# A hybrid retention and attention layer on one core: half of the projection's block pairs by seven products

## The chip, the cores and the metric

One core of a Trainium2 chip runs the whole layer. The metric is the device time of one execution in microseconds (us). TensorE multiplies matrices into the eight banks of PSUM, VectorE (DVE) and ScalarE (ACT) do elementwise work, GpSimd (POOL) and SyncE (SP) issue most DMAs.

## The reference

The input x has 256 rows (tokens) of 4096. It is normalised to h, and one product `proj = h @ w_in` gives 24,592 columns: q, k, v and gate of a retention branch (4 x 2048), q, k, v and gate of a forgetting attention (4 x 2048), 16 forget logits and 2 x 4096 merge gates. Then:

```
y_r = groupnorm(retention(rotary(q_r), rotary(k_r), v_r)) * silu(g_r)      (8 heads of 256)
y_f = softmax(q_f k_f^T / sqrt(128) + decay of the forget logits) v_f * silu(g_f)  (16 heads of 128)
merged = sigmoid(gate_0) * (y_r @ w_branch_ret) + sigmoid(gate_1) * (y_f @ w_branch_fox)
out = layernorm(2**0.25 * h + merged @ w_out)
```

All weights are float32: w_in is 403 MB, the two branch matrices 34 MB each, w_out 67 MB.

## The kernel before

Tokens lie on the output's partitions: two token tiles of 128. Every large product is cut into chunks of 512 columns, and a chunk into units of two blocks of 128 rows of weights (`KG = 2`), 512 KB each. `add_chunk` (line 100) lists the units of all chunks in the order of the work: 17 chunks of gate columns (the first with the forget logits, two narrow ones at the end), 16 chunks of retention (q, k, v, gate for each of four groups), 16 of forgetting attention, 16 of the two branch products, 8 of the output product.

The product is float32 in three rounded parts. `u_split` (line 116) makes of a raw weight block a high part (a copy that rounds, line 125, on ScalarE) and a low part (raw minus high, line 126, on VectorE). h has the parts hTh and hTl. `u_pe` (line 130) then issues for each block and token tile three matmuls of 512 columns into the same accumulator: high by high (line 144), low weight by high h (line 145), high weight by low h (line 146). A unit of full width is 2 x 2 x 3 = 12 matmuls.

`u_load` (line 110) loads a unit on SP's queue into one of five raw buffers. The split parts have four buffers of 128x512 each (`RING * KG`). `feed` (line 690) emits the splits of a unit once the unit two before it has its last step behind it. The emitted order is not the final one: when the program is built, each engine's queue is ordered by a list scheduler that takes the instruction that is ready. Where a run of units takes the token tiles one after the other (the first four and the last five units), `keep_for` (line 669) gives them other buffers.

In the first 16 units the input's normalisation, transposes and splits (`hT_part`, line 191) run between the units.

At the end of a chunk an evacuation takes the accumulator (two banks for both token tiles, two such pairs). For gates (line 248) it adds a bias, takes the sigmoid and stores to `gates_d` in device memory on POOL's queue. For q and k of retention it multiplies by cosine and sine (lines 297, 300) and combines (307, 308); for the others it copies. What remains of attention (transposes, scores, softmax or group norm, products) is written as Python generators in the list `bg`, and `bg_step` (line 151) runs one or two of their steps after each unit, so that attention of a group runs under the projection of the next. The merge chunks fetch gates from `gates_d`, multiply (lines 521, 531, 532), transpose; the output chunks add the residual, prepared in `pre` (lines 587 to 590), in `ev` (lines 596 to 601).

Four PSUM banks belong to the accumulators (`accp`), four to everything else (`psp`).

Of the kernel before, what the change touches and what calls it, by code (L numbers as in the profile page):

```python
# [8 lines left out]
F32 = mybir.dt.float32  # L9
# [15 lines left out]
KG = 2  # L25
EPS = 1e-5
ALPHA = 2.0 ** 0.25
BIG = 3.0e38


@with_exitstack
def hybrid_kernel(
# [16 lines left out]
    accp = ctx.enter_context(tc.tile_pool(name="accp", bufs=2, space=PS))  # L49
# [4 lines left out]
    cumT_d = dram.tile([FH, S], F32, name="cumT_d")  # L54

# [40 lines left out]
    units = []  # L96
    where = dict(w_in=0, w_branch_ret=0, w_branch_fox=0, w_out=0)
    RING, LOADS = 2, 5

    def add_chunk(wname, n, stat, evac, drain_at=None, pre=None, apart=False):  # L100
        ng = len(stat) // KG
        holder = {}
        for g in range(ng):
            size = KG * P * n
            w0 = where[wname]
            where[wname] += size
            units.append(dict(src=aps[wname][w0:w0 + size], n=n, stat=stat, g=g, ng=ng, evac=evac, h=holder,
                              drain=g == drain_at, pre=pre if g == 4 else None, keep=None, apart=apart))

    def u_load(u):  # L110
        n = u["n"]
        raw = wp.tile([P, KG * NC], F32, name="wraw", tag="wraw", bufs=LOADS)
        nc.sync.dma_start(raw[:, :KG * n], u["src"].rearrange("(p f) -> p f", p=P))
        u["raw"] = raw[:, :KG * n].rearrange("p (j n) -> p j n", j=KG)

    def u_split(u):
        n = u["n"]
        u["hi"], u["lo"] = [], []
        for j in range(KG):
            if u["keep"] is None:  # L120
                hi = wp.tile([P, NC], F32R, name="whi", tag="whi", bufs=RING * KG)
                lo = wp.tile([P, NC], F32R, name="wlo", tag="wlo", bufs=RING * KG)
            else:
                hi, lo = u["keep"][j]
            u["copy"] = nc.scalar.copy(hi[:, :n], u["raw"][:, j, :]).ins  # L125
            nc.vector.tensor_tensor(lo[:, :n], u["raw"][:, j, :], hi[:, :n].bitcast(F32), op=ALU.subtract)  # L126
            u["hi"].append(hi)
            u["lo"].append(lo)

    def u_pe(u, tiles):  # L130
        n, g = u["n"], u["g"]
        if "acc" not in u["h"]:
            a = accp.tile([P, T, NC], F32, name="acc", tag="acc")
            b = accp.tile([P, T, NC], F32, name="acc", tag="acc") if u["apart"] else a
            u["h"]["acc"], u["h"]["by"] = a, (a, b)
        by = u["h"]["by"]
        for j in range(KG):
            sh, sl, k = u["stat"][g * KG + j]
            first = g == 0 and j == 0
            last = g == u["ng"] - 1 and j == KG - 1  # L140
            for t in tiles:
                ts = slice(t * P, (t + 1) * P)
                o = by[t][:, t, :n]
                nc.tensor.matmul(o, lhsT=sh[:, k, ts], rhs=u["hi"][j][:, :n], start=first, stop=False)  # L144
                nc.tensor.matmul(o, lhsT=sh[:, k, ts], rhs=u["lo"][j][:, :n], start=False, stop=False)  # L145
                mm = nc.tensor.matmul(o, lhsT=sl[:, k, ts], rhs=u["hi"][j][:, :n], start=False, stop=last)  # L146
        return mm.ins
# [43 lines left out]
    def hT_part(blocks, t0, t1):  # L191
        """Transposes, scales, shifts and splits the given k blocks of token tiles t0..t1 (one bank)."""
# [55 lines left out]
    def gate_evac(a0, off, n):  # L248
        def f(acc):
# [3 lines left out]
            if off:  # L253
                fz = work.tile([P, T, FH], F32, name="fz", tag="fz", bufs=1)
                nc.vector.tensor_tensor(
                    fz, acc[:, :, 0:FH], bforg[:, None, :].to_broadcast([P, T, FH]), op=ALU.add
                )
                bg.append(forget_bg(fz))
            nc.vector.tensor_tensor(
                g[:, :, :n], acc[:, :, off:off + n], bb[:, None, :n].to_broadcast([P, T, n]), op=ALU.add  # L260
            )
# [7 lines left out]
    yrh = big.tile([P, 16, S], F32R, name="yrh", tag="yb0")  # L269
    yrl = big.tile([P, 16, S], F32R, name="yrl", tag="yb1")  # L270
# [13 lines left out]

    def ret_group(gi):
        st = {}

        def ev_rot(name):
            def f(acc):
                if not rscr:  # L290
                    rscr["ab"] = big.tile([P, 4, T, NC], F32, name="rab", tag="yb2")
                    rscr["ry"] = big.tile([P, 4, T, NC], F32, name="rry", tag="yb3")
                pi = 0 if name == "q" else 1
                A, B = rscr["ab"][:, 2 * pi], rscr["ab"][:, 2 * pi + 1]
                for t in range(T):
                    v = acc[:, t, :].rearrange("p (a b) -> p a b", b=P)
                    nc.vector.tensor_tensor(
                        A[:, t, :].rearrange("p (a b) -> p a b", b=P), v,
                        cos[:, t, None, :].to_broadcast([P, 4, P]), op=ALU.mult)
                    nc.vector.tensor_tensor(  # L300
                        B[:, t, :].rearrange("p (a b) -> p a b", b=P), v,
                        sin[:, t, None, :].to_broadcast([P, 4, P]), op=ALU.mult)
                R = rscr["ry"][:, pi].rearrange("p t (h x b) -> p t h x b", h=2, x=2)
                Av = A.rearrange("p t (h x b) -> p t h x b", h=2, x=2)
                Bv = B.rearrange("p t (h x b) -> p t h x b", h=2, x=2)
                for t in range(T):
                    nc.vector.tensor_tensor(R[:, t, :, 0, :], Av[:, t, :, 0, :], Bv[:, t, :, 1, :], op=ALU.subtract)
                    nc.vector.tensor_tensor(R[:, t, :, 1, :], Bv[:, t, :, 0, :], Av[:, t, :, 1, :], op=ALU.add)
                dst = work.tile([P, 4, S], F32, name=name, tag="at_" + name, bufs=1)
                st[name] = dst  # L310

                def cb(i0, ps):
                    nc.scalar.copy(dst[:, i0:i0 + 2, :], ps)

                bg.append(transpose_to(cb, lambda i, t: R[:, t, i // 2, i % 2, :], 4))
            return f

        def ev_v(acc):
            v = work.tile([P, T, NC], F32, name="v", tag="at_v", bufs=1)
            nc.scalar.copy(v, acc)  # L320
            st["v"] = v

        def ev_g(acc):
# [522 lines left out]
```

## Time and profile before

| | us |
|---|---|
| two runs | 2918.99 and 2919.61, median 2919.3 |
| span of the profiled execution | 2917.6 |
| median less that span | 1.7 |

The profile is of one execution. Its own time outside the span is not listed; the span and the 1.7 us up to the median stand for it. In the page and in what was asked of the trace, L12 is line 12 of the kernel, "out<-in" names tiles, a mean is that of one instruction, and "<-" behind an idle time names what ended it. Matmuls are pipelined: one is recorded at 0.39 us although the next begins earlier.

### The profile page before, as it was taken

The numbers are of one execution on the slowest core, as the hardware profiler recorded it, in microseconds if no ns is written. First come the engines' busy times: TensorE is split into PE (matmuls) and PEld (weight loads), VectorE is DVE, ScalarE is ACT, GpSimd is POOL, SyncE is SP. The second block draws the span as 40 slices with busy tenths as digits, with TensorE's granted clock in tenths as the row PEclk, the third lists the DMA queues.
The fourth block names the chain that finished last, engine by engine and source line by source line (L and its number), as shares of the span: only waits on it lengthen the run. The fifth ranks groups of instructions, "written<-read, shape, count | busy, mean of one in ns | idle before, by whom it ended". The sixth has DMA issues, their size and how long they took to land.

```text
span 2917.6 us, 37002 instructions
## 1 busy us (share of the span) xinstructions
PE 2888.2 (99%) x13146; PEld 2399.4 (82%) x13146; DVE 1689.5 (58%) x2622; ACT 1402.0 (48%) x2326; POOL 110.0 (4%) x198
## 2 busy tenths in 40 slices
PE   7999999999999999999999999999999999999998
PEld 5888888889888888888888888888888888888886
DVE  7555555555555555555555555555556656666666
ACT  5544444445444444444445454555455444444443
POOL 0000000000000000000000001000000000000000
PEclk9999999999999999999999999999999999999999
DMA  6666666666656566565666656666666666666674
GB/s 222 215 217 205 214 214 205 216 214 189 219 181 199 183 198 189 181 197 182 198 188 184 189 182 192 192 186 187 187 196 205 213 215 211 220 216 226 214 230 174
DMA packets 164394, 586.88 MB, mean 201 GB/s; under 512 B 19259, under 2 KB 19531, under 8 KB 164203
## 3 DMA queue, kind: packets, MB, share of 16 engines
q1 hardware_dynamic: 151632, 543.49, 57.7%
q0 software_dynamic: 12000, 38.93, 5.1%
q8 instruction: 102, 1.67, 0.2%
q10 hardware_dynamic: 576, 2.10, 0.2%
q14 instruction: 84, 0.69, 0.1%
HBM read 571.76 MB, written 12.68 MB: 200 GB/s over the span
## 4 chain that ended last, share of the span: by engine, by line
PE 98%; DVE 1%; DMA 1%; ACT 0%; issue 0%; SPq 0%; DVEq 0%; ACTq 0%
PE acc L146 32%; PE acc L145 32%; PE acc L144 32%; PE ps L279 1%; DMA x<-in_x 1%; DVE z L637 0%; DMA wraw<-in_w_out 0%; PE ps L434 0%; PE ps L345 0%; DVE wlo L126 0%; PE ps L200 0%; PE ps L451 0%; ACT whi L125 0%; PE ps L461 0%; PE ps L462 0%; PE ps L348 0%
## 5 line engine op out<-in xcount | busy, mean ns | idle before, releaser
L126 DVE TENSOR_TENSOR wlo<-wraw,whi 128x512 fp32r<-128x512 f32 (+2 forms) x2070 | 1406.3, 683 | 1152.8 <-ACT whi L125 1151.9
L125 ACT CAST whi<-wraw 128x512 fp32r<-128x512 f32 (+2 forms) x2070 | 1272.5, 617 | 1441.0 <-DVE wlo L126 1116.7
L145 PE MATMUL acc<-wlo,hTh 128*128 128x512 f32 (+2 forms) x3128 | 1214.6, 388 | 0.2 <-DVE wlo L126 0.2
L144 PE MATMUL acc<-whi,hTh 128*128 128x512 f32 (+2 forms) x3128 | 1210.4, 387 | 2.1 <-DVE hTh L206 2.1
L146 PE MATMUL acc<-whi,hTl 128*128 128x512 f32 (+2 forms) x3128 | 1205.2, 385 | 0.6 <-DVE rstd L91 0.6
L144 PEld LDWEIGHTS acc<-whi,hTh 128*128 128x128 f32 x3128 | 588.0, 188 | 119.7 <-ACT whi L125 2.5
L146 PEld LDWEIGHTS acc<-whi,hTl 128*128 128x128 f32 x3128 | 588.2, 188 | 116.3 <-DVE hTl L207 1.1
L145 PEld LDWEIGHTS acc<-wlo,hTh 128*128 128x128 f32 x3128 | 588.1, 188 | 115.9 <-DVE wlo L126 0.8
L145 PE MATMUL acc<-wlo,mTh 128*128 128x512 f32 x500 | 194.7, 389 | 0.4 <-DVE wlo L126 0.4
L146 PE MATMUL acc<-whi,mTl 128*128 128x512 f32 x500 | 194.5, 389 | 0.0
L144 PE MATMUL acc<-whi,mTh 128*128 128x512 f32 x500 | 191.5, 389 | 0.0
L145 PEld LDWEIGHTS acc<-wlo,mTh 128*128 128x128 f32 x500 | 93.9, 188 | 20.2 <-DVE wlo L126 0.7
L144 PEld LDWEIGHTS acc<-whi,mTh 128*128 128x128 f32 x500 | 93.9, 188 | 19.7 <-ACT whi L125 0.2
L146 PEld LDWEIGHTS acc<-whi,mTl 128*128 128x128 f32 x500 | 93.9, 188 | 19.2
L145 PE MATMUL acc<-wlo,yrh 128*128 128x512 f32 x256 | 100.3, 392 | 0.0
L144 PE MATMUL acc<-whi,yrh 128*128 128x512 f32 x256 | 99.7, 389 | 0.0
L146 PE MATMUL acc<-whi,yrl 128*128 128x512 f32 x256 | 99.6, 389 | 0.0
L144 PE MATMUL acc<-whi,yfh 128*128 128x512 f32 x256 | 99.6, 389 | 0.0
L145 PE MATMUL acc<-wlo,yfh 128*128 128x512 f32 x256 | 99.6, 389 | 0.0
L146 PE MATMUL acc<-whi,yfl 128*128 128x512 f32 x256 | 99.6, 389 | 0.0
L145 PEld LDWEIGHTS acc<-wlo,yfh 128*128 128x128 f32 x256 | 48.1, 188 | 10.0
L146 PEld LDWEIGHTS acc<-whi,yfl 128*128 128x128 f32 x256 | 48.1, 188 | 10.0
(205 smaller groups left out, 1026.5 us busy)
## 6 DMA issues: line engine op xcount, KB each, us to landing
wraw<-in_w_in SPq DMA_DIRECT2D x752, 512.0 KB, 4.0
wraw<-in_w_out SPq DMA_DIRECT2D x128, 512.0 KB, 4.3
wraw<-in_w_branch_ret SPq DMA_DIRECT2D x64, 512.0 KB, 4.2
wraw<-in_w_branch_fox SPq DMA_DIRECT2D x64, 512.0 KB, 3.4
g<-gates_d POOLq DMA_DIRECT2D x16, 512.0 KB, 5.4
gates_d<-g POOLq DMA_DIRECT2D x14, 512.0 KB, 5.5
wraw<-in_w_in SPq DMA_DIRECT2D x16, 272.0 KB, 3.0
wraw<-in_w_in SPq DMA_DIRECT2D x16, 256.0 KB, 3.1
```

The source lines that it names most:

```text
L125: u["copy"] = nc.scalar.copy(hi[:, :n], u["raw"][:, j, :]).ins
L126: nc.vector.tensor_tensor(lo[:, :n], u["raw"][:, j, :], hi[:, :n].bitcast(F32), op=ALU.subtract)
L144: nc.tensor.matmul(o, lhsT=sh[:, k, ts], rhs=u["hi"][j][:, :n], start=first, stop=False)
L145: nc.tensor.matmul(o, lhsT=sh[:, k, ts], rhs=u["lo"][j][:, :n], start=False, stop=False)
L146: mm = nc.tensor.matmul(o, lhsT=sl[:, k, ts], rhs=u["hi"][j][:, :n], start=False, stop=last)
L279: nc.tensor.transpose(ps[:, i, t * P:(t + 1) * P], src(i0 + i, t), ident)
```

## The change

The 16,384 projection columns are no longer taken in 32 chunks of 512 but in 16 double chunks of 1024, for both token tiles at once. For a pair of row blocks of the weights (256 rows), the 256 x 256 part of h and the 256 x 1024 part of the weights are each seen as 2 x 2 blocks. Eight of the 16 pairs take the usual eight block products. The other eight (`SEVEN`, alternating with them) take seven products of sums of blocks (the scheme of Strassen in Winograd's form): sums of blocks of h are made once (`make_sops`), sums of weight blocks in each unit on VectorE, and every sum is split again into high and low part. Each product is three matmuls as before. All eight PSUM banks hold the products of a double chunk, and an evacuation combines them (`proj_evac`) and stores the 256 x 1024 result to `proj_d` in device memory.

The order of the work changes: two gate chunks come first, then the double chunks with nothing beside them, then the other 15 gate chunks. Under these, attention fetches q, k, v and gate from `proj_d`. Raw buffers are three of 1 MB instead of five of 512 KB. The split buffers are two pairs of 128x1024, one for a whole unit (r0, r1); the double chunks use two more (a0, a1), and the sums of a seven-product unit have two sets of their own (t0, t1). Accumulators are single banks.

```diff
+FRONT = 2
+SEVEN = tuple(range(8, 16))
+PAIRS = tuple(p for i in range(8) for p in (i, 8 + i))
...
-    accp = ctx.enter_context(tc.tile_pool(name="accp", bufs=2, space=PS))
+    accp = ctx.enter_context(tc.tile_pool(name="accp", bufs=4, space=PS))
...
+    proj_d = dram.tile([S, 4 * RW + 4 * FW], F32, name="proj_d")
...
-    RING, LOADS = 2, 5
+    RAW = 3
...
+            units.append(dict(kind="c", ld=ld, part=g % 2, n=n, stat=stat, g=g, ng=ng, evac=evac, h=holder,
+                              drain=g == drain_at, pre=pre if g == 4 else None, keep=None,
+                              cands=(cands if cands and g < 2 else [("r0",), ("r1",)])))
...
+    SLOT = dict(r0=("wh0", "wl0"), r1=("wh1", "wl1"), a0=("at_q", "at_k"), a1=("at_v", "at_g"))
...
+    def split_into(hi, lo, src):
+        c = nc.scalar.copy(hi, src)
+        nc.vector.tensor_tensor(lo, src, hi.bitcast(F32), op=ALU.subtract)
+        return c.ins
 
     def u_split(u):
...
+            u["copy"] = split_into(hi[:, :w], lo[:, :w], raw[:, u["part"] * w:(u["part"] + 1) * w])
...
+        if not u["seven"]:
+            for i in range(2):
+                split_into(st[i][0], st[i][1], raw[:, 2 * i * NC:2 * (i + 1) * NC])
...
+        split_into(st[0][0], st[0][1], raw[:, NC:3 * NC])
+        ta = work.tile([P, 2, NC], F32, name="ta", tag="w4", bufs=2)
+        tb = work.tile([P, 2, NC], F32, name="tb", tag="w4", bufs=2)
+        nc.vector.tensor_tensor(ta, B[0][:, None, :].to_broadcast([P, 2, NC]),
+                                raw[:, NC:3 * NC].rearrange("p (a n) -> p a n", a=2), op=ALU.add)
+        nc.vector.tensor_tensor(tb[:, 0, :], ta[:, 0, :], B[2], op=ALU.add)
+        nc.vector.tensor_tensor(tb[:, 1, :], tb[:, 0, :], B[3], op=ALU.add)
+        split_into(st[1][0][:, :NC], st[1][1][:, :NC], B[3])
+        ts = big.tile([P, 2, 2, 2, NC], F32R, name="tset", tag="yb0" if u["slots"][2] == "t0" else "yb1")
+        for i, t_ in enumerate((ta, tb)):
+            split_into(ts[:, i, 0], ts[:, i, 1], t_)
...
+    def three(o, a, w, first, last):
+        nc.tensor.matmul(o, lhsT=a[0], rhs=w[0], start=first, stop=False)
+        nc.tensor.matmul(o, lhsT=a[0], rhs=w[1], start=False, stop=False)
+        return nc.tensor.matmul(o, lhsT=a[1], rhs=w[0], start=False, stop=last)
...
+    def pair_pe(u):
...
+            for k in ("1", "2", "6", "5"):
+                h["m"][k] = accp.tile([P, NC], F32, name="acc", tag="acc")
+            for k in ("3", "7", "4", "x"):
+                h["m"][k] = psp.tile([P, NC], F32, name="ps", tag="ps")
...
+            work_ = [("1", blk(0, 0), f["b11"]), ("2", blk(0, 1), f["b21"]), ("6", so(2), f["t2"]),
+                     ("5", so(1), f["t1"]), ("3", so(0), f["b22"]), ("7", so(3), f["t3"]), ("4", blk(1, 1), f["t4"])]
+        else:
+            b12, b11, b22, b21 = u["b"]
+            work_ = []
+            for k, t, c0, c1 in (("2", 0, b11, b21), ("3", 0, b12, b22), ("4", 1, b11, b21), ("x", 1, b12, b22)):
+                work_ += [(k, blk(t, 0), c0), (k, blk(t, 1), c1)]
...
+    def make_sops(hi, lo, pairs_, sops):
...
+            nc.vector.tensor_tensor(o[:, 1, :], a22, a21, op=ALU.subtract)
+            nc.vector.tensor_tensor(o[:, 3, :], a11, a21, op=ALU.subtract)
+            nc.vector.scalar_tensor_tensor(o[:, 2, :], o[:, 1, :], -1.0, a11, op0=ALU.mult, op1=ALU.subtract)
+            nc.vector.tensor_tensor(o[:, 0, :], a12, o[:, 2, :], op=ALU.add)
+            split_into(sh[:, n_], sl[:, n_], o)
+            yield
+
+    def proj_evac(c0):
...
+            nc.scalar.copy(a, m["1"])
+            op(c11, m["2"], a, ALU.add)
+            put(0, 0, c11)
+            op(a, m["6"], a, ALU.add)
+            op(v, m["5"], a, ALU.add)
+            op(c12, m["3"], v, ALU.subtract)
+            put(0, 1, c12)
+            op(a, m["7"], a, ALU.add)
+            op(v, m["7"], v, ALU.add)
+            op(a, m["4"], a, ALU.add)
+            put(1, 0, a)
+            op(v, m["x"], v, ALU.subtract)
+            put(1, 1, v)
...
+    def fetch(col, name, tag, bufs=1):
+        v = work.tile([P, T, NC], F32, name=name, tag=tag, bufs=bufs)
+        nc.gpsimd.dma_start(v, rows(proj_d, col, NC))
+        return v
...
+    sops = {p: None for p in SEVEN}
+    add_gates(gates[:FRONT])
+    first_pair = len(units)
+    for i in range(16):
+        add_pair("w_in", hTh, hTl, sops, PAIRS, proj_evac(2 * i * NC))
+    after_pairs = len(units)
+    add_gates(gates[FRONT:], [("a0",), ("a1",)])
...
+        if u["kind"] == "p":
+            cands = [("r0", "r1") if (i - first_pair) % 2 else ("a0", "a1")]
...
-        bg_step(1 if len(bg) < 3 else 2)
+        if s_ == 20:
+            bg.append(make_sops(hTh, hTl, SEVEN, sops))
+        if i == first_pair - 1:
+            bg_step(1000)
+        if i == after_pairs:
+            bg.extend(ret_group(gi) for gi in range(4))
+            bg.extend(fox_group(gi) for gi in range(4))
+        if u["kind"] == "c":
+            bg_step(1)
...
-    nc = bacc.Bacc("TRN2", target_bir_lowering=False, num_devices=1)
+    nc = bacc.Bacc("TRN2", target_bir_lowering=False, num_devices=1, dynamic_dma_scratch_size=8192)
```

## Rows read from the trace of the kernel before

**Rows 1.** The page's part 1: busy us, share of the span, instructions.
```profile
PE 2888.2 (99%) x13146; PEld 2399.4 (82%) x13146; DVE 1689.5 (58%) x2622; ACT 1402.0 (48%) x2326; POOL 110.0 (4%) x198
```
**Rows 2.** Waits, TensorE's own: us in total, times, longest us.
```profile
PE ps L200 <- DVE x L184: 16.8, 2, 15.7
...
PE acc L145 <- DVE wlo L126: 0.5, 2, 0.4
```
**Rows 3.** Timeline of a steady stretch: start us, us, instruction, idle before.
```profile
1002.75 0.39 PE L144 MATMUL acc<-whi,hTh 128*128 128x512 f32 x1
...
1003.20 0.39 PE L146 MATMUL acc<-whi,hTl 128*128 128x512 f32 x1
...
1003.43 0.39 PE L144 MATMUL acc<-whi,hTh 128*128 128x512 f32 x1
...
1003.63 0.62 ACT L125 CAST whi<-wraw 128x512 fp32r<-128x512 f32 x1 [0.74 <-PE acc L146]
```
**Rows 4.** VectorE's groups by line and shape: busy us, mean ns, idle before.
```profile
L126 DVE TENSOR_TENSOR wlo<-wraw,whi 128x512 fp32r<-128x512 f32 x2006 | 1378.7, 691 | 1133.4 <-ACT whi L125 1132.7
...
L589 DVE TENSOR_TENSOR xc<-xc,gb 128x1024 f32<-128x1024 f32 x8 | 9.8, 1219 | 0.0
```
**Rows 5.** Timeline of VectorE where a retention chunk is evacuated.
```profile
1001.56 0.69 DVE L126 TENSOR_TENSOR wlo<-wraw,whi 128x512 fp32r<-128x512 f32 x1 [0.67 <-ACT whi L125]
1002.27 0.69 DVE L297 TENSOR_TENSOR rab<-acc,cos 128x512 f32<-128x512 f32 x1
...
1004.67 0.69 DVE L126 TENSOR_TENSOR wlo<-wraw,whi 128x512 fp32r<-128x512 f32 x1
1005.27 0.42 DVE L307 TENSOR_TENSOR rry<-rab 128x256 f32<-128x256 f32 x1
1005.60 0.42 DVE L308 TENSOR_TENSOR rry<-rab 128x256 f32<-128x256 f32 x1
1005.94 0.69 DVE L126 TENSOR_TENSOR wlo<-wraw,whi 128x512 fp32r<-128x512 f32 x1
1006.54 0.42 DVE L307 TENSOR_TENSOR rry<-rab 128x256 f32<-128x256 f32 x1
...
1007.21 1.89 DVE L126 TENSOR_TENSOR wlo<-wraw,whi 128x512 fp32r<-128x512 f32 x3
```
**Rows 6.** ScalarE's groups by line and shape.
```profile
L125 ACT CAST whi<-wraw 128x512 fp32r<-128x512 f32 x2006 | 1246.1, 623 | 1419.5 <-DVE wlo L126 1115.5 <-PE acc L146 292.8 <-ACT whi L125 8.1
...
L125 ACT CAST whi<-wraw 128x256 fp32r<-128x256 f32 x32 | 13.0, 406 | 9.7 <-PE acc L146 8.8 <-DVE wlo L126 0.5 <-ACT whi L125 0.2
...
L400 ACT COPY nat<-acc 128x1024 f32<-128x1024 f32 x8 | 8.1, 1016 | 5.9 <-PE acc L146 5.9
```
**Rows 7.** Stretches: busy us of each engine (instructions), granted clock, DMA share, GB/s.
```profile
20.00:60.00 40.00, 38.19 (x186) 31.32 (x187) 35.77 (x68) 33.15 (x67) 0.67 (x1) 1.00 0.51 177
800.00:2210.00 1410.00, 1410.00 (x6414) 1170.96 (x6413) 796.68 (x1271) 684.28 (x1143) 48.55 (x93) 1.00 0.62 189
```
**Rows 8.** Timeline of ScalarE at a forgetting head.
```profile
1560.77 1.28 ACT L443 ACT_TABLE_LOAD   x1
...
1563.56 1.75 ACT L125 CAST whi<-wraw 128x512 fp32r<-128x512 f32 x3
```
**Rows 9.** The page's DMA issues: count, KB each, median us to landing.
```profile
wraw<-in_w_in SPq DMA_DIRECT2D x752, 512.0 KB, 4.0
...
g<-gates_d POOLq DMA_DIRECT2D x16, 512.0 KB, 5.4
```
**Rows 10.** Waits, VectorE for a fetched residual.
```profile
DVE xc L587 <- DMA xc<-in_x: 2.7, 4, 1.3
```
**Rows 11.** Timeline of VectorE where an output chunk is evacuated.
```profile
2595.39 1.29 DVE L596 SCALAR_TENSOR_TENSOR z<-xc,acc 128x512 f32<-128x512 f32 x2
2596.59 0.68 DVE L126 TENSOR_TENSOR wlo<-wraw,whi 128x512 fp32r<-128x512 f32 x1
2597.19 1.28 DVE L598 BATCH_NORM_STATS2 xst<-z 128x6 f32<-128x512 f32 x2
```
**Rows 12.** Stretches at the end of the run (columns as in rows 7).
```profile
2904.00:2906.00 2.00, 0.00 (x0) 0.00 (x0) 1.91 (x7) 0.00 (x0) 0.56 (x1) 1.00 0.41 170
...
2908.00:2911.00 3.00, 3.00 (x7) 1.16 (x5) 3.00 (x6) 0.00 (x0) 0.00 (x0) 0.50 0.98 397
```

More of the change, by code (lines that the diff above doesn't have):

```diff
@@ L103, in add_chunk @@
         for g in range(ng):
[L104 to L114, printed above, removed]
+            if g % 2 == 0:
+                loads.append(dict(n=n, srcs=[], users=0))
@@ new lines, in u_load, with w_tile @@
+    def u_load(ld):
+        raw = wp.tile([P, 4 * NC], F32, name="wraw", tag="wraw", bufs=RAW)
+        w = ld["srcs"][0].shape[0] // P
+        for i, src in enumerate(ld["srcs"]):
+            nc.sync.dma_start(raw[:, i * w:(i + 1) * w], src.rearrange("(p f) -> p f", p=P))
+        ld["raw"] = raw
+    SLOT = dict(r0=("wh0", "wl0"), r1=("wh1", "wl1"), a0=("at_q", "at_k"), a1=("at_v", "at_g"))
+    def w_tile(slot, i, n=2 * NC):
+        tag = SLOT[slot][i]
+        pool = wp if slot[0] == "r" else work
+        return pool.tile([P, n], F32R, name="wlo" if i else "whi", tag=tag, bufs=1)
@@ L142, in u_pe @@
                 ts = slice(t * P, (t + 1) * P)
[L143 to L146, printed above, removed]
+                mm = three(u["h"]["acc"][t][:, :n], (sh[:, k, ts], sl[:, k, ts]), u["w"][j], first, last)
+        return mm.ins
+    def pair_pe(u):
+        h, p, g = u["h"], u["p"], u["g"]
+        if "m" not in h:
+            h["m"] = {}
+            for k in ("1", "2", "6", "5"):
+                h["m"][k] = accp.tile([P, NC], F32, name="acc", tag="acc")
+            for k in ("3", "7", "4", "x"):
+                h["m"][k] = psp.tile([P, NC], F32, name="ps", tag="ps")
+            h["begun"] = set()
+        blk = lambda t, i: (u["hi"][:, 2 * p + i, t * P:(t + 1) * P], u["lo"][:, 2 * p + i, t * P:(t + 1) * P])
+        if u["seven"]:
+            sh, sl = u["sops"][p]
+            f = u["f"]
+            so = lambda i: (sh[:, i, :], sl[:, i, :])
+            work_ = [("1", blk(0, 0), f["b11"]), ("2", blk(0, 1), f["b21"]), ("6", so(2), f["t2"]),
[5 more added lines that the diff above has]
+                work_ += [(k, blk(t, 0), c0), (k, blk(t, 1), c1)]
+        for i, (k, a, w) in enumerate(work_):
+            more = (g + 1 < u["ng"]) and (g + 2 < u["ng"] or k != "x")
+            mm = three(h["m"][k], a, w, k not in h["begun"], not more and all(k != w_[0] for w_ in work_[i + 1:]))
+            h["begun"].add(k)
         return mm.ins
@@ L467, in attend @@
         def attend():
+            yield from turn("q", base)
+            yield from turn("k", base + FW)
+            st["v"] = fetch(base + 2 * FW, "v", "at_v")
+            g = fetch(base + 3 * FW, "gn", "w4", 2)
+            yield
+            sg = work.tile([P, T, NC], F32, name="sg", tag="at_g", bufs=1)
+            nc.scalar.activation(sg, g, AF.Sigmoid)
+            nc.vector.tensor_tensor(sg, sg, g, op=ALU.mult)
+            st["g"] = sg
+            yield
             yn = work.tile([P, T, NC], F32, name="yn", tag="w4", bufs=2)
@@ L831 @@
         if k == 'w_in':
[L832 removed]
+            give(k, w_in_tiles(lay[k]))
         elif k in ('w_branch_ret', 'w_branch_fox', 'w_out'):
```

300 lines of the change are left out of this document (173 added, 127 removed).

## The prediction

> **What bounds the kernel now.** I read the page's engine table first: TensorE is busy for 2888 of 2917.6 us, VectorE for 58% [rows 1]. Then TensorE's own waits: 16.8 us for the first normalised input, and after that almost nothing; in the whole run the weight split keeps it waiting for 0.5 us [rows 2]. So the kernel is as long as its list of matmuls, and two things count: how many matmuls go, and whether everything that feeds them still comes in time. The third view is the timeline of one steady stretch: three matmuls of 512 columns take 0.68 us from start to start, 0.2267 us each, and ScalarE begins the next split 0.04 us after the recorded end of the matmul that freed its buffer, that is 0.2 us after the next matmul has begun [rows 3].
>
> **What goes.** 16 double chunks have 8 seven-product pairs each, and every such pair has one block product of three matmuls less: 16 x 8 x 3 = 384 matmuls, 384 x 0.2267 = 87.0 us. All of it lies on TensorE's path. The transposes and attention products stay and only move under the gate columns. TensorE's list without any wait is 2917.6 - 87.0 = 2830.6 us.
>
> **What VectorE and ScalarE must do in the pair units.** One 512-wide subtraction is recorded at 691 ns and a 1024-wide operation at 1219 ns [rows 4], but back to back they start closer: three of L126 take 1.89 us, so 0.60 us from start to start, and the 256-wide pair 0.33 us [rows 5]. By the same 0.09 us of overlap a 1024-wide one costs 1.13 us. An eight-product unit has two 1024-wide low parts, 2.26 us. A seven-product unit has four 1024-wide operations (low parts of b11/b22 and of both t sets, and ta) and three of 512 (tb twice, b21): 4 x 1.13 + 3 x 0.60 = 6.32 us. Together 8.58 us in the 24 + 21 = 45 matmuls or 10.20 us of the two units. VectorE has 1.6 us to spare. ScalarE has five 1024-wide copies and one of 512. A 512-wide one is 623 ns, a 256-wide one 406 ns [rows 6], so 0.85 ns per element and some 1.06 us for 1024 (estimate from these two rows; the 1024-wide copy out of PSUM is 1.02): 5.9 us of 10.2.
>
> The order matters as much. The slots are single: the eight-product slot is free 0.2 us into the seven-product unit, then 1.06 us of copy and 1.13 of subtraction give the first low part at 2.5 of 4.76 us. The t sets have a slot of their own and wait only for raw weights, so 4.6 of the 6.32 us can fill VectorE's holes, if the queue is in that order. Rows 5 speak for it: L126 of the next unit stands between L307 and L307 of an older evacuation, so an operation that is ready goes ahead of an older one that isn't. I take no wait inside a double chunk.
>
> At its end the evacuation puts eight dependent 512-wide operations, 4.8 us, on VectorE while only 1.6 us are spare. Counted from the start of the last unit, VectorE then has 2.26 + 4.8 + 6.32 = 13.4 us to do, and the sixth product's low part of the next seven-product unit is wanted after 4.76 + 5.44 + 1.36 + 0.23 = 11.8: up to 1.7 us late. The banks come free in time: they are emptied in the order in which they end, one each 0.6 us, against 0.68 us per product. TensorE can meanwhile take products whose operands are there, since seven products sit in seven banks. Bounds 0 and 1.7 us per evacuation; I take 0.8 x 16 = 13 us.
>
> The Trainium skill speaks against this budget: "VectorE: DVE Perf Modes", section "The DRAIN you can't avoid", says that the next operation does not start until the pipe is empty. By that the two units would cost 6 x 1.22 + 3 x 0.69 = 9.4 us and an evacuation 5.5. Rows 5 disagree here (0.60 us from start to start of 0.69 us operations), so I go by the row; the rule's result is a rival below.
>
> **What the coarser ring costs everywhere else.** Before, a buffer is one 128x512 half: four of them, so a split has 4.08 us less its own 1.3 until it is needed, and rows 5 show it late by 1.75 us (L126 at 1004.67 in place of 1002.92) without a wait of TensorE. After, a buffer is a whole unit and there are two. Freed at 0.2 us, copy to 1.26, subtraction to 2.5; its first use is the second matmul of the next unit but one, at 2.72 + 0.23 = 2.95 us. The cover is 0.4 us in place of 2.8. Any VectorE or ScalarE work in front of a split that is longer than the 1.6 us hole between splits plus 0.4 us becomes a wait of TensorE. Place by place:
> - Start: the input's normalisation runs under the first units, VectorE busy 35.8 of 40 us there [rows 7]; and 8 sets of sums, about 2.3 us each, now follow in the second chunk (1.13 + 2.3 in a unit of 2.72). 12 units x 0.6 + 8 x 0.6 = 12 us (0 to 25).
> - Attention under 15 gate chunks. It has 4 x 19 + 4 x 23 = 168 steps, one per unit, in 240 units, so it ends before the merge. Each of 8 rotations puts four independent 0.6 us operations in a row (rows 5 show them unbroken): 2.4 us against 2.0, from the middle of a hole more, 0.9 us each, 7 us. ScalarE in the forgetting heads: a table load of 1.28 us and the exponentials hold the next copies until 1563.56, 2.8 us after 1560.77 [rows 8]; sigmoids of the gates now come between, so some 8 such switches at 1.0 us, 8 us. 16 heads at 0.25 us, 4 us. 32 fetches: the like transfer from gates_d lands in 5.4 us, twice a unit [rows 9], and the only sample of VectorE waiting for one, the xc fetch, waited 2.7 us over four times [rows 10]; 0.15 x 32 = 5 us. Sum 24 us (5 to 60).
> - Merge and output: the closing evacuation goes in pairs of 1.2 us with a split between [rows 11], so a split is late by about 0.9 us, 0.5 beyond cover, at 7 chunks, and at 8 merge chunks the sum behind the product costs 0.4: 7 us (0 to 25).
>
> **What is hidden.** POOL gets 64 stores and 32 fetches at 0.55 to 0.73 us of issue each, on an engine that is nearly idle; ScalarE loses 16 copies of q, k and v out of the accumulator, 1.02 us each; what queues behind a waiting fetch is the gate store and the next bias load, and the accumulators are double-buffered over a chunk of 43 us. SP's weight loads become 1 MB with three buffers; a buffer comes back three units (15 us) later, and the 512 KB load lands in 4.0 us [rows 9], so 6 to 7 us for twice the size (estimate) leaves margin. DMA engines are busy 0.62 in that stretch [rows 7]; stores and fetches add 34 MB over 2.9 ms, 12 GB/s on 189. Nothing for both; if it is wrong, up to 1 us in each of 16 double chunks.
>
> **The sum.** 2917.6 - 87.0 + 13 + 12 + 24 + 7 = 2886.6 us of span. The median of the runs, 2919.3, is 1.7 above that span; this is added: 2888 us. With every bound at its low end 2837 (none in the pairs, 5 under the gates), at its high end 2969 (27 + 25 + 60 + 25 against 87).
>
> **Rivals.**
> - Waits absorbed: the queues are ordered so well that hardly 14 us of waits remain. For it: before, late splits of 1.75 us cost nothing, and transposes of TensorE can fill holes. Against it: that cover was 2.8 us. 2919 - 87 + 14 = 2846 us.
> - The other side, VectorE in program order inside the seven-product unit. Place: the first subtraction there waits for the slot that the previous seven-product unit frees. If ta and tb stand behind it, VectorE begins at 0.2 + 1.06 = 1.3 us after that end and needs 6.32 us more, while the sixth product's low part is wanted 7.0 us after that end (5.44 of the unit between, two products and a matmul): 0.7 us late in each of 128 units, 90 us. It decides from (87 - 43) / 128 = 0.34 us per unit. 2888 + 90 - 13 = 2965 us. Against it: the mixed order of rows 5.
> - The drain as a mechanism: every VectorE operation holds its engine for its recorded length. 128 x 9.4 + 16 x 5.5 = 1290 us of work in 1306 us of matmuls; with even 0.4 us of idle per pair of units, 50 us more: 2938 us. That is the rule of the Trainium skill above; the trace's 0.60 us is against it.
> - A gap that lowers the clock: after the wait of 3.1 us at the end the granted clock is 0.50, that is 1.2 GHz [rows 12]. The gaps that I expect are under 2 us, so I give it nothing; a few longer ones would cost some 3 us each and lie inside the range.
> - The products stay: then 13,146 TensorE instructions would not fall to 12,762. The code leaves no doubt, 0.
>
> **How the numbers follow.** My forecast of 2888 us (own range 2861 to 2919) gets 0.56, waits absorbed 0.27, program order 0.11, the drain 0.06. About 2% (58 us; 2861 and 2978) is what a measurement of this kernel can tell from no change. Below 2861 lie the absorbed case and a little of the forecast's edge: 0.29. Above 2978 half of the program-order case: 0.06. Within: 0.65. The range leaves out some 0.1 at each side: 2843 to 2955 us.
>
> **What would show it.** Right: 12,762 TensorE instructions; VectorE's busy time up by about 510 us (128 x 9.4 + 88 in the pairs against 1024 x 0.69 before, less 85 in the other units); waits of TensorE for the splits in small pieces, most under the gates and at the 16 evacuations; none inside a double chunk. Wrong: TensorE waiting 0.3 us or more in every seven-product unit (order or drain), for raw weights (loads), or for the fetched rows in pieces of over 2 us.

## The result, and the profile after

The changed kernel takes 3001.9 us (two runs, 2998.4 and 3005.35) against 2919.3: ratio 1.028, 95% interval 1.025 to 1.031. The forecast was 2888 us, 2843 to 2955: wrong, and on the wrong side, since the change makes the kernel slower. The span of the profiled execution is 2996.6 us, 79.0 more than before. Three lines of the page (parts 1, 5 and 6):

```profile
PE 2874.9 (96%) x12762; PEld 2344.4 (78%) x12762; DVE 2132.5 (71%) x2432; ACT 1373.8 (46%) x1550; POOL 165.2 (6%) x294
...
L175 DVE TENSOR_TENSOR ta<-wraw 128x1024 f32<-128x1024 f32 x128 | 156.8, 1225 | 181.4 <-DMA wraw<-in_w_in 180.9
...
wraw<-in_w_in SPq DMA_DIRECT2D x256, 1024.0 KB, 4.9
```

Beside [rows 1], the 384 matmuls are gone (13,146 to 12,762), yet TensorE's busy time fell by only 13.3 us, not 87.0, and 121.7 us of the span are now idle where 29.4 were. A busy time that falls less than its instructions do points to matmuls that run slower; how much of that the clock explains is worked out below. VectorE's busy time rose by 443 us (510 were forecast). TensorE's own waits, longest sums first (us in total, times, longest us):

```profile
PE acc L190 <- DVE wlo L148: 36.4, 41, 3.5
PE acc L189 <- DVE ev L378: 25.3, 15, 2.5
PE ps L288 <- DVE x L272: 17.0, 2, 15.8
PE ps L406 <- DVE rry L441: 4.8, 1, 4.8
PE acc L189 <- DVE ea L378: 9.2, 9, 1.1
PE acc L189 <- ACT ea L381: 8.2, 9, 2.3
```

The start (L288) is that of [rows 2]. New are the waits for the low parts (L148) and for operations of the evacuation (L378, L381), some 15 evacuations' worth. To place them, the first and last starts of marks that stand once per chunk (line, operation, count: shortest/mean/longest ns, first to last start):

```profile
L381 ACT COPY ea<-acc x16: 567/576/589, 207.9 to 1552.4; 128x512 f32<-128x512 f32 x16
...
L650 DVE TENSOR_TENSOR m<-acc,g x16: 680/681/684, 2290.9 to 2602.4; 128x512 f32<-128x512 f32 x16
...
L726 DVE SCALAR_TENSOR_TENSOR z<-xc,acc x16: 678/681/689, 2668.7 to 2981.6; 128x512 f32<-128x512 f32 x16
```

The nearest marks of the kernel before (its gate evacuations, its first merge evacuation, its output evacuations; a semaphore row stands 0.7 us ahead of the operation that waits there, so differences between the two tables are good to about 1 us):

```profile
L259 DVEq EVENT_SEMAPHORE  x16: 21/50/50, 118.5 to 731.3; - x16
...
L521 DVEq EVENT_SEMAPHORE  x8: 21/21/21, 2217.6 to 2528.5; - x8
...
L596 DVE SCALAR_TENSOR_TENSOR z<-xc,acc x16: 680/684/689, 2595.4 to 2902.6; 128x512 f32<-128x512 f32 x16
```

- Start and first double chunk: 207.9 us, against 118.5 for two gate chunks and 81.6 for the matmuls of a double chunk (8 x 45 x 0.2267, [rows 3]): 7.8 us lost.
- The next 15 double chunks, with the fifteen evacuations between them: (1552.4 - 207.9) / 15 = 89.6 us each, 8.0 more than their matmuls: 120.5 us.
- Gate columns with attention under them, from the last copy of L381 to the first merge evacuation: 738.5 us. The work of that stretch took, before, 731.3 - 118.5 = 612.8 us (15 gate chunks) and 93.5 (attention and the first merge chunk: 2217.6 - 731.3 less 32 chunks of 192 x 0.2267). So 32.2 us are lost. The sixteenth evacuation is among them, but TensorE has only two gaps beside it (1.11 us before 1560.31, 0.37 before 1566.46) and the granted clock stays at 1.00.
- Merge 377.8 us, as before. Output to the end 327.9 against 322.2: 5.7 us.

7.8 + 120.5 + 32.2 + 5.7 = 166.2 us are lost, 87.2 are gained (1392.8 of 32 chunks against 16 x 81.6), and 79.0 is the difference of the spans. What happens at the end of a double chunk is seen in VectorE's timeline there:

```profile
928.10 0.68 DVE L378 TENSOR_TENSOR e<-acc,ea 128x512 f32<-128x512 f32 x1
928.70 1.82 DVE L148 TENSOR_TENSOR wlo<-wraw,whi 128x512 fp32r<-128x512 f32 x2
930.44 1.22 DVE L148 TENSOR_TENSOR tset<-tb,tset 128x1024 fp32r<-128x1024 f32 x1
931.57 0.68 DVE L378 TENSOR_TENSOR ea<-acc,ea 128x512 f32<-128x512 f32 x1
933.50 1.23 DVE L175 TENSOR_TENSOR ta<-wraw 128x1024 f32<-128x1024 f32 x1 [1.24 <-DMA wraw<-in_w_in]
934.64 0.68 DVE L378 TENSOR_TENSOR ev<-acc,ea 128x512 f32<-128x512 f32 x1
...
940.58 0.68 DVE L378 TENSOR_TENSOR ev<-ps,ev 128x512 f32<-128x512 f32 x1
```

The eight operations of the evacuation (L378) are torn apart: splits of the next units stand between them, and an addition (L175) waits 1.24 us for raw weights at the head of the queue while the third evacuation operation, whose inputs are there, stands behind it. The evacuation takes 928.10 to 941.26, 13.2 us, where 4.8 were counted. TensorE in the same place (timeline, then stretches of 2 us: busy us, granted clock in the third column from the end):

```profile
932.40 0.47 PE L189 MATMUL acc<-tset,soh 128*128 128x512 f32 x1 [1.09 <-DVE ea L378]
...
935.38 0.79 PE L189 MATMUL acc<-tset,soh 128*128 128x512 f32 x1 [2.04 <-DVE ev L378]
```

```profile
930.00:932.00 2.00, 0.91 (x3) 0.30 (x2) 2.00 (x3) 0.00 (x0) 0.00 (x0) 1.00 0.94 369
932.00:934.00 2.00, 0.94 (x3) 0.49 (x3) 0.76 (x2) 0.42 (x1) 0.00 (x0) 1.00 0.98 401
934.00:936.00 2.00, 0.62 (x2) 0.52 (x3) 2.00 (x4) 1.24 (x2) 0.00 (x0) 0.71 0.85 360
936.00:938.00 2.00, 2.00 (x6) 1.36 (x5) 2.00 (x4) 0.00 (x0) 0.54 (x1) 0.50 0.00 0
938.00:940.00 2.00, 2.00 (x6) 1.52 (x6) 2.00 (x4) 0.51 (x1) 0.00 (x0) 0.50 0.33 131
```

All eight PSUM banks belong to the products, so until a bank is read out the next double chunk can't begin its product. TensorE is busy for 2.47 of the 6 us from 930 to 936. Near their end, in the gap of 2.04 us, the granted clock falls to 0.50 (the 0.71 is the mean of its stretch), and then 6 matmuls run in 2 us in place of 9. So one torn evacuation is paid twice, as gaps and as half speed behind them. Over all double chunks:

```profile
126.00:1556.00 1430.00, 1363.68 (x5763) 1097.66 (x5762) 1202.86 (x1278) 719.87 (x786) 35.79 (x65) 0.97 0.55 200
```

1430 us hold 66.3 of idle time and 1363.7 of busy time, and 5763 matmuls of 0.2267 are 1306.5, so 57 us of the busy time are lost too. Added up in stretches of 10 us, what the granted clock lacks of 1.00 is 44 us, in fifteen places, one per evacuation between double chunks. The other 13 us lie at the edges of the gaps: the matmul ahead of one is recorded to its end at 0.39 us, and the next after the first behind one comes later than 0.2267 us (0.31 after 932.40). The parts together are the 123 us by which this stretch is longer than its matmuls.

### The profile page after: what moved, and what is told of

Same layout as the page of the kernel before. It is cut to its first block, busy times and chain, and to the rows that moved or that the text cites. A ratio compares the mean times of both kernels' runs of the same rounds, so it can differ in the third digit from the quotient of the medians.

```text
span 2996.6 us, 33423 instructions
## 1 busy us (share of the span) xinstructions
PE 2874.9 (96%) x12762; PEld 2344.4 (78%) x12762; DVE 2132.5 (71%) x2432; ACT 1373.8 (46%) x1550; POOL 165.2 (6%) x294
## 4 chain that ended last, share of the span: by engine, by line
PE 48%; DVE 21%; DMA 20%; issue 9%; ACT 1%; POOL 0%; DVEq 0%; SPq 0%; ACTq 0%; POOLq 0%
DMA wraw<-in_w_in 18%; PE acc L190 14%; PE acc L189 14%; PE acc L191 14%; DVE wlo L148 8%; DVE tset L148 4%; DVE ta L175 2%; DVE tb L177 2%; DVE tb L178 2%; PE ps L189 1%; PE ps L190 1%; PE ps L191 1%; ACT whi L147 1%; DMA gates_d<-g 1%; PE ps L406 1%
## 5 line engine op out<-in xcount | busy, mean ns | idle before, releaser
L148 DVE TENSOR_TENSOR wlo<-wraw,whi 128x1024 fp32r<-128x1024 f32 (+2 forms) x1035 | 1161.8, 1139 | 574.7 <-ACT whi L147 573.7
L147 ACT CAST whi<-wraw 128x1024 fp32r<-128x1024 f32 (+2 forms) x1035 | 1001.9, 985 | 1142.5 <-PE acc L191 790.5
L190 PE MATMUL acc<-wlo,hTh 128*128 128x512 f32 (+2 forms) x1592 | 619.0, 391 | 34.8 <-DVE wlo L148 33.7
L191 PE MATMUL acc<-whi,hTl 128*128 128x512 f32 (+2 forms) x1592 | 607.9, 384 | 0.0
L189 PE MATMUL acc<-whi,hTh 128*128 128x512 f32 (+2 forms) x1592 | 564.9, 387 | 13.6 <-ACT ea L381 8.2
L190 PEld LDWEIGHTS acc<-wlo,hTh 128*128 128x128 f32 x1592 | 300.7, 189 | 112.9 <-DVE wlo L148 58.1
L189 PEld LDWEIGHTS acc<-whi,hTh 128*128 128x128 f32 x1592 | 296.0, 189 | 78.4 <-ACT ea L381 12.2
L191 PEld LDWEIGHTS acc<-whi,hTl 128*128 128x128 f32 x1592 | 301.2, 189 | 54.7 <-DVE hTl L295 0.3
L190 PE MATMUL ps<-wlo,hTh 128*128 128x512 f32 x768 | 303.6, 395 | 0.0
L191 PE MATMUL ps<-whi,hTl 128*128 128x512 f32 x768 | 301.9, 395 | 0.0
L175 DVE TENSOR_TENSOR ta<-wraw 128x1024 f32<-128x1024 f32 x128 | 156.8, 1225 | 181.4 <-DMA wraw<-in_w_in 180.9
L148 DVE TENSOR_TENSOR tset<-ta,tset 128x1024 fp32r<-128x1024 f32 x128 | 155.9, 1218 | 0.0
L148 DVE TENSOR_TENSOR tset<-tb,tset 128x1024 fp32r<-128x1024 f32 x128 | 155.8, 1217 | 0.0
```

The lines of the kernel that those rows point to most:

```text
L147: c = nc.scalar.copy(hi, src)
L148: nc.vector.tensor_tensor(lo, src, hi.bitcast(F32), op=ALU.subtract)
L175: nc.vector.tensor_tensor(ta, B[0][:, None, :].to_broadcast([P, 2, NC]), raw[:, NC:3 * NC].rearrange("p (a n) -> p a n", a=2), op=ALU.add)
L189: nc.tensor.matmul(o, lhsT=a[0], rhs=w[0], start=first, stop=False)
L190: nc.tensor.matmul(o, lhsT=a[0], rhs=w[1], start=False, stop=False)
L191: return nc.tensor.matmul(o, lhsT=a[1], rhs=w[0], start=False, stop=last)
```

## The experiments

The theory: the time is lost because work for later units goes ahead of the evacuation's operations on VectorE. Rivals: VectorE has too much to do there; ScalarE or the banks are too slow; the coarse split ring is the cause; seven products are not worth it. Each kernel is the changed kernel with the edit shown; ratios are against the kernel before, run beside it (2919.7 to 2920.4 us). Differences to the changed kernel are taken from its median of 3001.9, and its two runs lie 7 us apart.

**Held unit.** The split of the second unit of a double chunk, the seven-product one, is issued behind the evacuation's last operation.

```diff
-            op(v, m["x"], v, ALU.subtract)
+            state["evac"] = op(v, m["x"], v, ALU.subtract).ins
...
-            u_split(u)
+            if u["kind"] == "p" and u["g"] == 1 and "evac" in state:
+                with tc.issue_after(state["evac"]):
+                    u_split(u)
+            else:
+                u_split(u)
```

> Only VectorE's queue changes: the splits of the first seven-product unit of each double chunk are queued behind the last operation of the evacuation before it. Theory A (the eight banks come free late because splits and a sum that waits for raw weights stand between the evacuation's operations, and the gap then lowers the clock): a double chunk falls from 89.6 us to 82 to 85 us, TensorE's waits for ea and ev go, the granted clock in the pairs rises from 0.97 to 0.99 or more, time 2900 to 2935 us. Rival B (VectorE simply has too much work around an evacuation, in whatever order): the wait moves to the splits of that unit, a double chunk stays above 88 us, time within 15 us of the changed kernel's 3002.

Measured 2918.0 us, 0.9994 (0.9983 to 1.0005): 84 us gained with not one operation less. Its double chunk takes (1467.6 - 206.6) / 15 = 84.1 us, 2.5 more than its matmuls. TensorE no longer waits for an operation of the evacuation, and no stretch of the double chunks has a clock under 0.99; it waits mainly for sums, twice at each boundary:

```profile
L381 ACT COPY ea<-acc x16: 579/579/580, 206.6 to 1467.6; 128x512 f32<-128x512 f32 x16
...
PE acc L189 <- ACT tset L147: 15.5, 16, 2.1
...
PE ps L189 <- ACT tset L147: 4.9, 15, 0.3
```

The edit adds an order on VectorE alone, but TensorE's queue is ordered anew with it when the program is built: in the changed kernel products of the second unit's sums (932.40, 935.38) are among the first behind the boundary, here they come after the first unit's. This run doesn't separate the two queues; the last one does.

**All eight products copied out by ScalarE**, so that the banks come free without VectorE, which then combines the copies.

```diff
...
+            for i, k in enumerate(("1", "2", "6", "5", "3", "7", "4", "x")):
+                m[k] = (b_ if k in "4x" else w)("e" + k)
+                nc.scalar.copy(m[k], src[k])
...
```

> ScalarE copies all eight products out of PSUM (8 x 0.58 us per double chunk) and VectorE combines the copies in SBUF, in the same order of work otherwise. Theory A: banks come free within about a microsecond of their last matmul, so the double chunk falls to 82 to 84 us, the clock stays, time 2890 to 2920 us, although VectorE does as many operations as before. Rival B (VectorE's amount of work): no gain, the waits are for the split's low parts, time 2980 to 3010 us.

2933.3 us, 1.0045 (1.0029 to 1.0061), 13 above the band. It takes the banks out of the torn queue and gains 69 of the 84. What stays in the double chunks are mainly two short waits for low parts at most boundaries (L148: 21.7 us in 28, of 37.9 in 41 in the whole run).

**Split ring of the column chunks in halves**, as it was before.

```diff
-            u["copy"] = split_into(hi[:, :w], lo[:, :w], raw[:, u["part"] * w:(u["part"] + 1) * w])
+            r0 = u["part"] * w
+            u["copy"] = split_into(hi[:, :n], lo[:, :n], raw[:, r0:r0 + n])
+            split_into(hi[:, n:w], lo[:, n:w], raw[:, r0 + n:r0 + w])
```

> Only in the units of gate, branch and output chunks: a unit's split goes in two halves of 512 columns in the same buffers, so that the first low part is there about 1 us earlier. If the coarse ring is what costs about 32 us under the gates (738 us from the last double chunk to the first merge product against 706 worked out from before) and 6 us in the output chunks, 15 to 30 us of it go: 2970 to 2987 us. Rival (late fetched rows, VectorE and TensorE waiting for the attention's DMAs): no change within 5 us. The pairs stay as they are under both.

2979.6 us, 1.020 (1.017 to 1.023): 22 us, all outside the double chunks (last copy of the evacuation at 1555.8, first merge evacuation at 2275.0: 719.2 us in place of 738.5; output 323.7 in place of 327.9).

**Eight products everywhere**: no seven-product pair, four accumulators taken in turn, plain copies as evacuation.

```diff
-SEVEN = tuple(range(8, 16))
+SEVEN = ()
...
```

> All 16 pairs take eight products (SEVEN empty, no sums), the four results have four banks, so two double chunks alternate in the eight banks; everything else as in the changed kernel. TensorE has 13,146 instructions again. Theory A: the double chunks take 87.0 us each with no gap and full clock, and what remains against the kernel before is the part under the gates and at the end: 2950 to 2965 us, faster than the changed kernel by 40 to 50 although it does 384 matmuls more. Rival C (the double chunk's larger loads, the single slots or the stores to device memory cost the time): it stays 80 us or more above what its matmuls need, 3030 us or more.

2963.2 us, 1.0144 (1.0115 to 1.0174). 384 matmuls more and 39 us faster than the changed kernel. Its double chunk takes (1511.2 - 205.6) / 15 = 87.0 us, which is what its 16 x 24 matmuls need (384 x 0.2267), so the larger loads, the single slots and the stores to device memory cost nothing there:

```profile
L381 ACT COPY e<-acc x16: 587/589/589, 205.6 to 1511.2; 128x512 f32<-128x512 f32 x16
```

This prices the two halves of the change: the move of attention and the coarse units cost 43 us, and the seven products, which should give 87 back, cost 39 more as they stand.

**Both edits**, held unit and halves.

> The changed kernel with both edits: the last weights split of each double chunk's second unit held behind the evacuation, and the column chunks' splits in halves. If evacuation order and coarse splits are two separate costs in two separate stages (double chunks, and gate, merge and output chunks), their gains add: 2918.0 less 22.3 = 2896 (2888 to 2904), under the kernel before by about 24. Rival: with the order mended the coarse splits no longer matter, because their late tiles were an after-effect of the double chunks' lost time: 2913 to 2921.

2891.1 us, 0.9906 (0.9892 to 0.9921). The gains add, 84 and 27: two separate costs in two stages.

**Which instruction blocks?** Only the first addition of that unit (and so what depends on it) is held; its splits stay free. The evacuation's last operation is marked as in the held unit.

```diff
...
+        with ExitStack() as held:
+            if u["g"] == 1 and "evac" in state:
+                held.enter_context(tc.issue_after(state["evac"]))
+            nc.vector.tensor_tensor(ta, B[0][:, None, :].to_broadcast([P, 2, NC]),
...
```

> Only the first addition (ta) of the first set of sums after the evacuation is held behind the evacuation's last operation; the splits of the same unit stay free to go ahead of evacuation operations. If it is the addition that waits for raw weights at the head of VectorE's queue that blocks the evacuation, this alone gives nearly all of the held unit's gain: 2915 to 2930. If the splits that go between the evacuation's operations matter as much, it gives half or less: 2955 to 2985.

2934.7 us, 1.0052 (1.0037 to 1.0067): between the two bands. Holding the addition and what follows from it brings 67 of the 84 us, holding the splits as well the other 17.

**A shorter hold**: the held unit, but behind the fourth of the evacuation's eight operations on VectorE in place of the eighth. (The text below calls it the fifth; that counts ScalarE's copy too.)

```diff
-            op(c12, m["3"], v, ALU.subtract)
+            state["evac"] = op(c12, m["3"], v, ALU.subtract).ins
...
```

> As the held unit, but held only behind the fifth of the evacuation's eight operations (by which the banks of products 1, 2, 6, 5 and 3 are free), so that the unit's splits start about 2 us sooner. The held unit left waits of TensorE for that unit's sums of 16 times about 1 us; if holding too long is what is left of the boundary, this gains on it: 2900 to 2912. If the last banks (7, 4 and x) are what TensorE needs first, the blocked evacuation is back in part: 2930 to 2980. If neither, 2916 to 2921.

2924.1 us, 1.0019 (1.0009 to 1.0028): 6 us worse than the full hold, between the band of no effect (to 2921) and that of a blocked evacuation (from 2930). The waits for sums fall (15.5 to 11.3 us) and those for low parts double (15.1 to 29.5).

**All three**: held unit, halves, ScalarE's copies.

> Held unit, halves, and all eight products copied out by ScalarE. Copying by ScalarE frees all banks within about 5 us of the last matmul, which the held order alone does in about 6; so it should add nothing to e5 and costs ScalarE 7 more copies: equal to e5 within 8 us, so 2890 to 2904. Rival: the banks are still late in e5, then 10 to 20 less than e5; or ScalarE's copies delay its casts, then 10 to 20 more.

2902.3 us, 0.9939 (0.9922 to 0.9955): 11 us more than without the copies. It lies within 2890 to 2904, but not within 8 us of the run without copies, so the second rival fits better: the copies delay ScalarE's casts (TensorE's waits for high parts 9.5 us in 18, against 3.8 in 5).

**Amount or order?** Each double chunk begins with two eight-product units, so that VectorE has far less to do beside the evacuation. Nothing is held.

```diff
-PAIRS = tuple(p for i in range(8) for p in (i, 8 + i))
+PAIRS = (0, 1, 8, 2, 9, 3, 10, 4, 11, 12, 5, 13, 6, 14, 7, 15)
```

> The changed kernel with another order of the pairs alone: each double chunk begins with two eight-product units (0, 1, 8, 2, 9 ...), so that VectorE has only 2 x 2.3 us of splits beside the evacuation in 10.9 us of matmuls; the two seven-product units that then stand side by side are in the middle, with no evacuation near. Nothing is held back. If the cost is the seven-product unit's VectorE work meeting the evacuation, most of it goes: 2915 to 2940. If it is that the queue's order puts any work ahead of the evacuation, whichever it is, less than a third goes: 2975 to 3000.

2994.2 us, 1.0256 (1.024 to 1.0271): against the changed kernel nothing that the intervals separate, and inside the second band, that of the queue's order. The work is there early all the same, since the sums of the third unit have a slot of their own and need only raw weights. VectorE's timeline:

```profile
918.32 1.22 DVE L175 TENSOR_TENSOR ta<-wraw 128x1024 f32<-128x1024 f32 x1
919.46 0.68 DVE L378 TENSOR_TENSOR e<-acc,ea 128x512 f32<-128x512 f32 x1
920.06 2.35 DVE L148 TENSOR_TENSOR wlo<-wraw,whi 128x1024 fp32r<-128x1024 f32 x2
922.33 0.68 DVE L177 TENSOR_TENSOR tb<-ta,wraw 128x512 f32<-128x512 f32 x1
922.93 0.68 DVE L378 TENSOR_TENSOR ea<-acc,ea 128x512 f32<-128x512 f32 x1
923.53 1.21 DVE L148 TENSOR_TENSOR tset<-ta,tset 128x1024 fp32r<-128x1024 f32 x1
924.66 0.68 DVE L178 TENSOR_TENSOR tb<-tb,wraw 128x512 f32<-128x512 f32 x1
925.26 0.68 DVE L378 TENSOR_TENSOR ev<-acc,ea 128x512 f32<-128x512 f32 x1
```

**That order with halves.**

> As e9 with the column chunks' splits in halves. The halves gave 22 us on the changed kernel and 27 on the held one, so e9 less 22 to 27. With e9 at 2915 to 2940: 2890 to 2915.

2962.0 us, 1.0142 (1.0127 to 1.0157): 32 us less than without halves, more than the 22 to 27 expected; the absolute band missed as the one above did.

**That order with halves, second unit held.**

> As e10, and the second unit's split held behind the evacuation as in e5. In e5 TensorE still waits 16 times, about 1.3 us, for the held unit's sums; here the held unit is an eight-product one with no sums, 2.3 us of VectorE: those waits should go and nothing come in their place, 2865 to 2880. Rival: the two adjacent seven-product units (12.6 us of VectorE in 10.9 us of matmuls) cost as much in the middle of each double chunk, 16 x 1 to 2 us: 2888 to 2905.

2957.8 us, 1.0126 (1.011 to 1.0143), no difference that its interval separates from the run above. The same hold that gave 84 us gives nothing on an eight-product unit: the sums of the third unit are still free, and TensorE waits for the evacuation's fourth operation 15 times, 69.2 us. The miss names what is left to hold.

**The third unit held too.** The edit is shown against the run above.

```diff
-            if u["kind"] == "p" and u["g"] == 1 and "evac" in state:
+            if u["kind"] == "p" and u["g"] in (1, 2) and "evac" in state:
```

> As e11, but the splits of the second and of the third unit (the first one with seven products, whose additions went between the evacuation's operations in e9 and e11) are both held behind the evacuation. If the order of the queue is the whole of the boundary's cost, the 69 us of waits for the evacuation's fourth operation go, and the waits for the held unit's sums of e5 (16 times 1.3 us) do not come back, because two eight-product units stand before it: 2865 to 2880. Rival: the two adjacent seven-product units or the held third unit's sums cost 1 to 2 us in each of 16 double chunks: 2885 to 2905. If the order is not the cause, it stays at e11's 2958.

2867.0 us, 0.9816 (0.98 to 0.9833): 91 us from one more held unit, 135 under the changed kernel and 53 under the kernel before. TensorE's waits for the fourth operation, in the run above and here:

```profile
PE ps L191 <- DVE e L380: 69.2, 15, 5.8
...
PE ps L191 <- DVE e L380: 7.7, 15, 0.5
```

TensorE's own order across a boundary is the same in both but for a few instructions, and it stands before the same product, so these 91 us come from VectorE's order. Its timeline now has the evacuation in one piece:

```profile
947.54 0.68 DVE L380 TENSOR_TENSOR e<-acc,ea 128x512 f32<-128x512 f32 x1
948.31 0.69 DVE L380 TENSOR_TENSOR ea<-acc,ea 128x512 f32<-128x512 f32 x1
949.04 0.69 DVE L380 TENSOR_TENSOR ev<-acc,ea 128x512 f32<-128x512 f32 x1
...
951.62 0.68 DVE L380 TENSOR_TENSOR ea<-ps,ea 128x512 f32<-128x512 f32 x1
952.22 0.68 DVE L380 TENSOR_TENSOR ev<-ps,ev 128x512 f32<-128x512 f32 x1
952.82 2.35 DVE L148 TENSOR_TENSOR wlo<-wraw,whi 128x1024 fp32r<-128x1024 f32 x2
```

4.7 us from the first start to the last, against 12.5 in the changed kernel. TensorE there and over nearly all of the double chunks (5678 of 5760 matmuls), and the mark of the chunks:

```profile
950.00:952.00 2.00, 1.47 (x7) 1.22 (x7) 2.00 (x4) 0.00 (x0) 0.54 (x1) 1.00 0.90 334
952.00:954.00 2.00, 2.00 (x10) 1.65 (x10) 2.00 (x4) 0.00 (x0) 1.08 (x2) 1.00 0.84 336
...
126.00:1428.00 1302.00, 1292.27 (x5678) 1063.95 (x5677) 1183.89 (x1263) 716.43 (x775) 33.77 (x62) 1.00 0.59 217
```

```profile
L383 ACT COPY ea<-acc x16: 577/579/580, 203.4 to 1440.9; 128x512 f32<-128x512 f32 x16
```

One gap of half a microsecond is left at each boundary, the clock stays at 1.00, and a double chunk takes 82.5 us.

## Why the prediction was wrong, and where it was right

**The step that failed is the evacuation's term**, "0.8 x 16 = 13 us" with bounds 0 and 1.7 us each. It measured 8.0 us at each of the fifteen boundaries between double chunks, 120.5 in all, nearly five times the upper bound. The term added up VectorE's work (13.4 us of it against 11.8 of cover) and took for granted that the eight operations run as a block, "emptied in the order in which they end, one each 0.6 us". The runs show in its place that the order of VectorE's queue comes first: with two eight-product units at the start, so 4.1 us less work beside the evacuation (6.32 - 2.26), nothing was gained, and with the same work put in order 91 us.

The amount was undercounted too. With the order of pairs that the prediction reckoned with, the held unit still leaves 84.1 - 81.6 = 2.5 us each, mainly around late sums. So some 5.5 of the 8.0 us are the order, and the rest, above the bound of 1.7, is the amount of work or the hold itself, which no run separates (a shorter hold was worse). Only in the last run, with less work beside the evacuation, is it 82.5 - 81.6 = 0.9 us, 14 us for 16. That this is close to the 13 us of the term is luck: it is another order of pairs.

**The sign of [rows 5] was misread.** There an operation that was ready stood ahead of an older one that wasn't, and the prediction used it against the rival "program order". The same habit puts the next units' sums, which need only raw weights, ahead of the evacuation. Before, such a mixing cost nothing (0.5 us of waits for low parts in the whole run, [rows 2]). There an evacuation held two of four accumulators; now it holds all eight banks. With eight products everywhere it holds four of eight, and again nothing is lost; but that run has no sums that could go ahead either, so the number of banks is an argument and not shown by itself.

**The raw weights.** "Nothing for both" was wrong at this place. The 1 MB load lands in 4.9 us, sooner than the estimate of 6 to 7, but VectorE stands waiting for one 112 times, 1.6 us on average. Inside a double chunk that costs nothing: apart from the first one, TensorE has no gap there. At its end the waiting addition holds up the evacuation: the queue's order is fixed when the program is built, and the engine doesn't go past a waiting instruction. The Trainium skill says the same, "PSUM — Partial Sum Buffer", section "Engine vs sequencer instructions": VectorE's queue is strictly first in, first out. The row at 933.50 agrees, with 1.24 us. What the waiting alone costs is not separated from the mixing: at 918.32 in the run with two eight-product units first, the addition goes ahead of the evacuation without a wait, and that run gains nothing.

**The clock.** The rival "a gap that lowers the clock" got nothing because single gaps under 2 us were expected. At the boundary shown, four gaps of 0.4 to 2.0 us with matmuls between them were enough. Some 44 of the 123 us are the clock's, some 3 us per boundary, which is the price that the prediction named for a longer gap.

**Right**: the 87.0 us (the matmuls of the last run's double chunks take no longer than counted, and the boundaries keep 14 us); no wait inside a double chunk, but for two in the first one (2.07 and 0.96 us); start and gate columns together 7.8 + 32.2 = 40 us for 12 + 24, with whatever the sixteenth evacuation costs; merge and output 5.7 for 7. The coarse ring accounts for most of these, since halves give 22 to 32 us back; the single items of the 24 us (rotations, table loads, heads, fetches) were not measured one by one. With 120.5 us in place of 13 the prediction's own sum is 2996 us, against 2998.4 for the profiled execution.

**Sums of the prediction that are off**, without weight for the result: 13.4 - 11.8 is 1.6 us late and not 1.7; program order is 1.3 + 6.32 - 7.0 = 0.6 us late and not 0.7, so some 10 us less; the drain has 1290 + 51 - 1306 = 35 us and not 50; the terms for VectorE's busy time give 500 us and not 510, where 443 were measured.

**Two rivals.** The drain is out: in the block of the last run, operations that don't touch the tile of the one just before start 0.60 us apart (951.62 to 952.22, each 0.68 long), as in [rows 5]; the one at 949.04, which takes what the one before it has made, 0.73 us. The measurement is against the rule of the Trainium skill as the prediction cited it; but "The DRAIN you can't avoid" there ("VectorE: DVE Perf Modes") goes on that an operation that is not held starts earlier, which the prediction left out. The rival on the other side gave 2965 us by a VectorE queue in a bad order, but in the wrong place (inside the double chunk, where TensorE has no gaps) and for the opposite reason: too much order there, too much mixing here.

## What to carry to other kernels

Where one evacuation holds all banks, its operations can be the critical path: put them ahead of work for later units by an explicit dependency, and only then look at how much work it is. Budget a boundary by its queue order first (here some 5.5 of 8.0 us) and by the sum of its operations second, and add to its gaps what a fall of the clock behind them costs (here 44 us on 66 of idle time). When an ordering edit does nothing, look for the next piece of early work that is still free to go ahead.

## What was not expected of the hardware

The granted clock fell to 0.50 (1.2 GHz) behind gaps of 0.88, 0.40, 1.09 and 2.04 us with matmuls between them (928 to 935.4); before, it was seen only behind one gap of 3.1 us [rows 12]. A gap as long as the last of these four, in the first double chunk and with none shortly before it, left the clock at 1.00 in every stretch of 2 us from 136 to 150. In the last run a single gap of 0.53 us left it at 1.00 too.

```profile
139.87 0.73 PE L189 MATMUL acc<-tset,soh 128*128 128x512 f32 x2 [2.07 <-ACT tset L147]
```
